# A convolution with max pooling: the first casting load doubled to half an image, and the hand-written program order laid out anew

## The chip, the core and the metric

The kernel runs on one core of a Trainium2 chip. The metric is device time in microseconds (us) of one execution. Five engines work side by side, each through its own list of instructions in order: PE (matrix multiply; PEld is its weight load), DVE (vector), ACT (scalar), POOL (GpSimd) and SP, which here only issues DMA transfers. POOL issues transfers too. They meet through semaphores. PE writes its results to PSUM, of which this kernel has eight banks in two sets of four.

## The reference

A 3x3 convolution with padding 1 over 16 images of 64 channels and 64x64 pixels to 128 channels, and a 2x2 maximum over the result:

```python
batch, c_in, h, w, c_out, k = 16, 64, 64, 64, 128, 3
for each b, co, ci, kh, kw:
    conv[b, co] += weight[co, ci, kh, kw] * x_pad[b, ci, kh:kh+h, kw:kw+w]
output[b, c, i, j] = np.max(conv[b, c, 2*i:2*i+2, 2*j:2*j+2])
```

All inputs and outputs are float32; the kernel multiplies in bfloat16.

## The kernel before

**Tiles.** Images are taken two at a time: the 64 channels of one lie in partitions 0 to 63, those of the other in 64 to 127 (h is 0 or 1 below). A pair of images is cut into four chunks of 16 rows, each giving 8 pooled rows. There are 32 chunks, of two kinds, in an order fixed by `SEQ`: 14 of kind K and 18 of kind W. The vertical maximum needs an upper and a lower row of the convolution. In both kinds the kernel splits them into a part that both share and two remainders: it takes the maximum of the remainders and adds the shared part after that.

**Kind K** holds x in bfloat16 (tiles `kx`, a whole pair of images each, three buffers). Its products are PAa and PAb (first remainder), PBa and PBb (second remainder) and PR (shared part). Only PR needs a tile made beforehand, `KS` (sum of two rows, DVE). **Kind W** holds x in float32 (tiles `wx`, three buffers of four chunks) and needs four row tiles: S (sum, DVE), Z and Y (differences, POOL) and E (a difference: `E.i` makes it on DVE, `e.i` on POOL). Its products are P2 and P0 (first remainder), P3 (second) and P1 (shared part). After P2, `SE` on ACT seeds the second remainder's bank with the negated first one.

**A product** is three matmuls of 64x128 weights with 8x64 columns, for one h. Two products, one for each h, are issued interleaved, and they run at the same time on the two halves of PE. The order holds 142 such pairs; 852 matmuls in all.

**After the products** of a chunk: EV/ev (ACT) copies the first remainder out of PSUM, MX/mx (DVE) takes the maximum of it and the second, in the second's bank, PR or P1 is added there, OD/od (ACT) copies odd columns out, CM/cm (DVE) takes the maximum over columns into the tile `o`, and with the second h SP stores it. Capital letters stand for K, small ones for W. A PSUM bank goes back to its set after EV/ev or CM/cm, and the next product that needs a bank takes the one given back first in program order.

**Loads.** `wload` (L110 to L117, issued by SP) brings a W chunk as it is, 480 to 576 KB. `kload` (L104 to L108, issued by POOL) brings K chunks and casts to bfloat16 on the way. The first two K chunks are instead loaded in float32 by SP (`kfirst` L124, `ksecond` L335) and cast on DVE (XO, XE) and ACT (X1 and X2, L344). In the order `LD.i` is the load of W chunk i and `L0`, `L1`, ... the next casting load. Before, L0 is chunk 2 alone, L1 chunk 3 alone, and L2 to L6 are half images of two chunks each. SP issues loads and stores in one list, so a load waits behind the stores that stand ahead of it, and these for their CM/cm.

**The order** is written out by hand in `ORDER`: every engine gets its instructions in the order in which the names stand there. A name's *slot*, below, is the number of product pairs that stand ahead of it. Two rules add waits: a row tile on POOL waits for the DVE row operation that stands last ahead of it (`on_gpsimd`), and LD.1, LD.2, LD.3 wait for GM, E.0, E.1 (`load_w`), as ksecond waits for D2. At the start the 3x3 weights are combined (g0 to GP), turned by PE (T...) and copied to `wt` (V...).

Of the kernel before, what the change touches and what calls it, by code (L numbers as in the profile page):

```python
# [11 lines left out]
def kernel(  # L12
# [370 lines left out]


    ORDER = """
        g2 D0 D2 g1 TD0 GS g0 TD2 KX2 VD0 TG2 VD2 TG0 L0 VG2 TG1 XO GM VG0 PAa.0.0+PAa.0.1 XE LD.1 TGM GP
# [4 lines left out]
        P1.0.0+PAb.2.1 MX.1.0 SE.1.1 LD.3 P0.1.0+PBa.2.1 LD.4 EV.2.1 L2 E.2 P3.1.0+PBb.2.1 od.0.0 ev.1.0 S.1
        PR.1.0+P0.1.1 cm.0.0 Z.2 PAa.2.0+P2.2.1 MX.2.1 OD.1.0 ev.1.1 P2.2.0+P3.1.1 mx.1.0 Y.2 SE.2.1 CM.1.0
        PAb.2.0+PR.2.1 mx.1.1 SE.2.0 P1.1.0+P0.2.1 OD.2.1 E.3 EV.2.0 P0.2.0+P1.1.1 S.2 ev.2.1 P3.2.0+P3.2.1
        ev.2.0 CM.2.1 Y.3 PAa.3.0+PBa.1.1 od.1.0 mx.2.1 od.1.1 PAb.3.0+PAa.3.1 cm.1.0 Z.3 cm.1.1
        PBa.2.0+P1.2.1 mx.2.0 EV.3.0 PBb.2.0+PAb.3.1 LD.6 S.4 LD.5 P1.2.0+PBb.1.1 KS.3 Y.4 PAa.4.0+PBa.3.1
        od.2.0 MX.1.1 EV.3.1 PAb.4.0+PBb.3.1 cm.2.0 e.4 MX.2.0 P2.3.0+PR.1.1 EV.4.0 MX.3.1 PBa.3.0+PAa.4.1
        od.2.1 OD.1.1 Z.4 cm.2.1 SE.3.0 PBb.3.0+PAb.4.1 CM.1.1 PR.2.0+PR.3.1 EV.4.1 MX.3.0 P0.3.0+P2.3.1
        KS.4 OD.2.0 OD.3.1 CM.2.0 PR.3.0+PBa.4.1 L3 SE.3.1 S.3 P2.4.0+PBb.4.1 OD.3.0 CM.3.1 Z.5 ev.3.0
        CM.3.0 P3.3.0+P0.3.1 MX.4.1 SE.4.0 PBa.4.0+P2.4.1 LD.8 ev.3.1 S.6 P0.4.0+P3.3.1 LD.7 e.5 mx.3.0
        SE.4.1 PBb.4.0+PR.4.1 ev.4.0 mx.3.1 P3.4.0+P0.4.1 Y.6 MX.4.0 P1.3.0+P3.4.1 ev.4.1 mx.4.0  # L400
        PAa.5.0+P1.3.1 Z.6 od.3.0 mx.4.1 OD.4.1 PR.4.0+P2.5.1 cm.3.0 CM.4.1 PAb.5.0+P1.4.1 Y.5 OD.4.0 od.3.1
        CM.4.0 P2.5.0+PAa.5.1 od.4.1 cm.3.1 EV.5.0 P1.4.0+PAb.5.1 cm.4.1 SE.5.0 E.6 PBa.5.0+PBa.5.1 od.4.0
        KS.5 SE.5.1 cm.4.0 P0.5.0+PBb.5.1 EV.5.1 S.8 P2.6.0+P0.5.1 ev.5.0 LD.9 S.5 PBb.5.0+P2.6.1 SE.6.0 Z.7
        MX.5.1 P3.5.0+P3.5.1 ev.5.1 MX.5.0 P0.6.0+PR.5.1 SE.6.1 mx.5.0 e.7 PR.5.0+P3.6.1 ev.6.0 mx.5.1
        P1.5.0+P0.6.1 OD.5.1 Y.7 OD.5.0 CM.5.1 P2.7.0+P1.5.1 CM.5.0 od.5.0 ev.6.1 cm.5.0 PAa.6.0+PAa.6.1 L4
        KS.6 od.5.1 SE.7.0 PAb.6.0+P2.7.1 mx.6.1 Z.8 cm.5.1 P3.6.0+PAb.6.1 EV.6.0 P0.7.0+P1.6.1 S.9 EV.6.1
        LD.10 PBa.6.0+PBa.6.1 e.8 mx.6.0 od.6.1 SE.7.1 P3.7.0+PBb.6.1 cm.6.1 ev.7.0 PBb.6.0+P0.7.1 S.7 Y.8
        MX.6.1 PAa.7.0+P2.8.1 ev.7.1 mx.7.0 P1.6.0+P3.7.1 SE.8.1 MX.6.0 Y.9 PAb.7.0+PR.6.1 od.6.0 mx.7.1
        P1.7.0+P0.8.1 OD.6.1 cm.6.0 Z.9 PR.6.0+P3.8.1 CM.6.1 od.7.0 ev.8.1 cm.7.0 P2.8.0+P1.7.1 LD.11 EV.7.0
        mx.8.1 PAa.8.0+PAa.7.1 OD.6.0 SE.8.0 CM.6.0 PAb.8.0+P1.8.1 KS.8 od.7.1 KS.7 P0.8.0+PAb.7.1 od.8.1  # L410
        E.10 EV.8.0 PBa.7.0+PBa.7.1 Z.10 cm.8.1 ev.8.0 cm.7.1 PBb.7.0+PBb.7.1 EV.7.1 P2.10.0+PAa.8.1 MX.7.0
        e.9 LD.12 P3.8.0+P2.10.1 MX.7.1 SE.10.0 PR.7.0+PAb.8.1 Y.10 SE.10.1 mx.8.0 P0.10.0+PR.7.1 OD.7.0
        EV.8.1 CM.7.0 P1.8.0+P0.10.1 S.10 OD.7.1 L5 ev.10.0 P2.9.0+PBa.8.1 CM.7.1 od.8.0 S.11
        P3.10.0+PBb.8.1 ev.10.1 cm.8.0 PBa.8.0+P2.9.1 Z.12 MX.8.1 SE.9.0 PBb.8.0+P3.10.1 mx.10.0 LD.13
        SE.9.1 e.11 P3.9.0+PR.8.1 MX.8.0 P0.9.0+P3.9.1 mx.10.1 OD.8.1 Z.11 PR.8.0+P0.9.1 CM.8.1 ev.9.0
        P1.10.0+P1.10.1 mx.9.0 ev.9.1 e.12 PAa.9.0+P2.11.1 mx.9.1 od.10.1 od.10.0 PAb.9.0+PAa.10.1 OD.8.0
        cm.10.1 cm.10.0 P1.9.0+PAb.10.1 EV.9.0 KS.11 KS.9 PBa.9.0+PBa.10.1 EV.10.1 CM.8.0 Y.11
        P2.11.0+P1.9.1 od.9.0 SE.11.1 cm.9.0 PBb.9.0+PBb.10.1 od.9.1 Y.13 SE.11.0 cm.9.1 PAa.10.0+P0.11.1
        MX.10.1 PAb.10.0+P2.12.1 ev.11.1 LD.15 KS.10 MX.9.0 P0.11.0+P3.11.1 LD.14 e.13 SE.12.1
        P3.11.0+PR.10.1 ev.11.0 mx.11.1 PR.9.0+P0.12.1 L6 OD.10.1 EV.10.0 Z.13 CM.10.1 PBa.10.0+P1.11.1  # L420
        mx.11.0 OD.9.0 PBb.10.0+PAa.9.1 od.11.1 CM.9.0 ev.12.1 Y.12 cm.11.1 P1.11.0+PAb.9.1 MX.10.0
        P2.12.0+PAa.11.1 od.11.0 EV.9.1 cm.11.0 PR.10.0+PAb.11.1 S.13 SE.12.0 P2.13.0+P3.12.1 OD.10.0 Y.14
        EV.11.1 CM.10.0 P0.12.0+P2.13.1 mx.12.1 SE.13.0 P3.12.0+PBa.9.1 LD.16 ev.12.0 S.12 P0.13.0+PBb.9.1
        SE.13.1 e.14 mx.12.0 PAa.11.0+P1.12.1 MX.9.1 P1.12.0+P0.13.1 S.14 od.12.1 P3.13.0+PR.9.1 Z.14
        cm.12.1 od.12.0 ev.13.0 cm.12.0 PAb.11.0+P3.13.1 ev.13.1 P2.14.0+PBa.11.1 e.15 OD.9.1 mx.13.1
        EV.11.0 PBa.11.0+P2.14.1 CM.9.1 SE.14.0 mx.13.0 PBb.11.0+PBb.11.1 Y.15 SE.14.1 LD.17 P0.14.0+P1.13.1
        MX.11.0 P3.14.0+P0.14.1 Z.16 MX.11.1 ev.14.0 PR.11.0+P3.14.1 ev.14.1 mx.14.0 e.16 P1.13.0+PR.11.1
        od.13.1 mx.14.1 OD.11.0 P1.14.0+PAa.12.1 CM.11.0 od.13.0 cm.13.1 Z.15 P2.15.0+P1.14.1 cm.13.0
        od.14.0 OD.11.1 cm.14.0 PAa.12.0+P2.16.1 od.14.1 CM.11.1 Y.16 SE.15.0 PAb.12.0+PAb.12.1 cm.14.1
        PBa.12.0+PBa.12.1 EV.12.0 S.16 P0.15.0+PBb.12.1 EV.12.1 S.15 P2.16.0+PAa.13.1 SE.16.1 KS.12 ev.15.0  # L430
        PBb.12.0+PAb.13.1 e.17 MX.12.1 SE.16.0 P3.15.0+P0.16.1 MX.12.0 EV.13.1 Z.17 P0.16.0+P3.16.1 ev.16.1
        mx.15.0 P3.16.0+P2.17.1 ev.16.0 mx.16.1 Y.17 P1.15.0+PR.12.1 SE.17.1 mx.16.0 PR.12.0+P1.16.1 OD.12.1
        od.15.0 CM.12.1 PAa.13.0+P0.17.1 OD.12.0 cm.15.0 od.16.1 PAb.13.0+P3.17.1 S.17 ev.17.1 cm.16.1
        P1.16.0+P2.15.1 EV.13.0 KS.13 CM.12.0 P2.17.0+PBa.13.1 od.16.0 mx.17.1 SE.15.1 PBa.13.0+PBb.13.1
        cm.16.0 SE.17.0 PBb.13.0+P0.15.1 MX.13.1 P0.17.0+P3.15.1 ev.15.1 MX.13.0 P3.17.0+P1.17.1 mx.15.1
# [59 lines left out]
```

## Time and profile before

| | us |
|---|---|
| three timed runs | 114.47, 114.31, 111.48 |
| their median | 114.31 |
| the profiled execution, its own time | 112.98 |
| span of the profiled execution, first to last instruction | 111.2 |
| time that lies around the span (112.98 - 111.2) | 1.78 |

In the profile a line such as "L263 DVE TENSOR_TENSOR ws<-wx" names the code line, the engine, the operation and the tiles (output, arrow, inputs). Names in the profile are those of tiles: `ws`, `wz`, `wy`, `we` and `ks` are the row tiles S, Z, Y, E/e and KS; `o` is CM/cm; L302 is MX/mx. Busy time is not a bound by itself: what counts is where PE, which does the least avoidable work, stands still, and for what.

### The profile page before, as it was taken

What the parts mean: (1) busy time and instruction counts of PE and PEld (TensorE: products, weight loads), DVE (VectorE), ACT (ScalarE), POOL (GpSimd) and SP (SyncE); (2) the same over time, 40 slices, a digit from 0 to 9 for tenths busy, and PEclk for the clock granted to TensorE, in tenths of its full rate; (3) what the DMA queues carried; (4) which work ended last, traced back from release to release, by engine and by line L of the source; (5) the groups of instructions that cost most, each with busy time, mean ns of one, the idle gap of its engine ahead of it and who ended that gap; (6) DMA issues with size and microseconds to landing.
All of it is one profiled execution on the core that took longest, in us unless ns stands there. A gap on an engine that the chain in (4) does not pass through costs nothing.

```text
span 111.2 us, 2480 instructions
## 1 busy us (share of the span) xinstructions
PE 100.8 (91%) x889; PEld 50.2 (45%) x889; DVE 92.2 (83%) x177; ACT 79.4 (71%) x173; POOL 67.6 (61%) x76
## 2 busy tenths in 40 slices
PE   7997999999999988799999998299999999999930
PEld 2552355544444433355568552144444454555400
DVE  0597489889999996999998898238989999989960
ACT  4574698864797796587797957097896877989640
POOL 6329137826947960995938649386918999690000
PEclk9999999999999999999999999999999999999999
DMA  3989937897899999549988889739699595400534
GB/s 89 352 212 221 320 67 152 221 273 221 245 304 126 281 359 304 173 110 143 316 182 278 205 113 268 262 113 168 212 262 291 223 215 218 136 0 6 189 140 143
DMA packets 12781, 22.55 MB, mean 203 GB/s; under 512 B 992, under 2 KB 9312, under 8 KB 12768
## 3 DMA queue, kind: packets, MB, share of 16 engines
q1 hardware_dynamic: 11760, 19.24, 55.1%
q0 software_dynamic: 1008, 3.15, 18.1%
q8 instruction: 7, 0.11, 0.5%
q14 instruction: 6, 0.05, 0.2%
HBM read 17.14 MB, written 8.39 MB: 230 GB/s over the span
## 4 chain that ended last, share of the span: by engine, by line
PE 39%; DMA 17%; DVE 9%; POOL 3%; issue 2%; ACT 1%; SPq 0%; DVEq 0%; POOLq 0%
PE acc L213 39%; DMA wx<-in_x_dram 8%; DMA kx<-in_x_dram 8%; DVE acc L302 3%; DVE ws L263 3%; DVE o L315 2%; POOL wz L263 1%; POOL we L263 1%; POOL wy L263 1%; DVE ks L263 1%; ACT od L306 1%; DVE we L263 1%; SPq L327 0%; DVEq L490 0%; POOLq L263 0%
## 5 line engine op out<-in xcount | busy, mean ns | idle before, releaser
L213 PEld LDWEIGHTS <-wt 64*128 64x128 bf16 x852 | 46.8, 94 | 51.6 <-issue 5.9
L213 PE MATMUL acc<-kx,wt 64*128 64x512 bf16 (+3 forms) x336 | 62.0, 374 | 3.6 <-DMA kx<-in_x_dram 2.6
L293 ACT COPY ev<-acc 128x512 f32<-128x512 f32 x64 | 36.7, 596 | 11.0 <-PE acc L213 10.6
L302 DVE TENSOR_TENSOR acc<-acc,ev 128x512 f32<-128x512 f32 x64 | 42.1, 692 | 2.7 <-PE acc L213 1.3
L263 POOL TENSOR_TENSOR wz<-wx 128x512 bf16<-128x512 f32 x18 | 23.4, 1302 | 18.6 <-DVE we L263 6.4
L213 PE MATMUL acc<-we,wt 64*128 64x504 bf16 (+1 forms) x108 | 28.4, 376 | 0.8 <-DVE o L315 0.8
L263 POOL TENSOR_TENSOR wy<-wx 128x512 bf16<-128x512 f32 x18 | 23.5, 1309 | 8.7 <-DVE ws L263 3.1
L213 PE MATMUL acc<-wz,wt 64*128 64x504 bf16 (+1 forms) x108 | 28.1, 377 | 0.0
L306 ACT COPY od<-acc 128x256 f32<-128x256 f32 x64 | 22.8, 382 | 7.4 <-PE acc L213 7.0
L315 DVE TENSOR_TENSOR o<-acc,od 128x256 f32<-128x256 f32 x64 | 24.7, 416 | 3.6 <-ACT od L306 3.2
L213 PE MATMUL acc<-ws,wt 64*128 64x504 bf16 (+1 forms) x108 | 26.7, 377 | 0.1
L213 PE MATMUL acc<-wy,wt 64*128 64x504 bf16 (+1 forms) x108 | 26.0, 377 | 0.0
L298 ACT ACTIVATE acc<-acc 128x512 f32<-128x512 f32 x36 | 21.0, 589 | 4.5 <-PE acc L213 2.3
L213 PE MATMUL acc<-ks,wt 64*128 64x504 bf16 (+1 forms) x84 | 20.2, 377 | 0.7 <-DVE acc L302 0.7
L263 DVE TENSOR_TENSOR ws<-wx 128x512 bf16<-128x512 f32 x18 | 15.9, 891 | 1.3 <-DMA wx<-in_x_dram 1.3
L263 POOL TENSOR_TENSOR we<-wx 128x512 bf16<-128x512 f32 x12 | 15.3, 1272 | 2.6 <-DVE ks L263 2.0
L263 DVE TENSOR_TENSOR ks<-kx 128x512 bf16<-128x512 bf16 x14 | 6.3, 462 | 3.5 <-DMA kx<-in_x_dram 2.9
L263 DVE TENSOR_TENSOR we<-wx 128x512 bf16<-128x512 f32 x6 | 5.5, 909 | 0.9 <-DMA wx<-in_x_dram 0.9
L442 PE MATMUL acc<-const-bfloat16-1.0 128*128 128x512 bf16 x8 | 3.6, 625 | 0.8 <-PEq L476 0.8
L108 POOL DMA_DIRECT2D kx<-in_x_dram x7 | 4.3, 610 | 0.0
L174 PEld LDWEIGHTS <-wq 128*128 128x128 bf16 x28 | 2.2, 120 | 1.6 <-issue 1.2
L174 PE MATMUL acc<-ident,wq 128*128 128x128 bf16 x28 | 2.7, 263 | 0.0
(28 smaller groups left out, 15.5 us busy)
## 6 DMA issues: line engine op xcount, KB each, us to landing
out_dram<-o SPq DMA_DIRECT2D x30, 256.0 KB, 4.5
wx<-in_x_dram SPq DMA_DIRECT2D x8, 512.0 KB, 6.8
wx<-in_x_dram SPq DMA_DIRECT2D x5, 480.0 KB, 5.8
wx<-in_x_dram SPq DMA_DIRECT2D x4, 544.0 KB, 6.0
kx<-in_x_dram POOLq DMA_DIRECT2D x3, 528.0 KB, 8.1
...
```

What stands on the lines that cost most here:

```text
L108: nc.gpsimd.dma_start(out=ktile(i)[:, lo:hi, :], in_=rows_of(p, lo, hi))
L174: nc.tensor.transpose(tp[:, (j - lo) * 128 : (j - lo + 1) * 128], wq[:, j : j + 2, :].rearrange("a b c -> a (b c)"), ident,)
L213: lambda kw=kw, o0=o0, o1=o1, c0=c0, c1=c1: nc.tensor.matmul(dst[:, i0:i1, o0:o1], wt[lo : lo + CI, m0 + kw - h, :], rows(lo, i0, i1, c0, c1),
L263: return engine.tensor_tensor(out=r, in0=t[:, f + a : f + a + 2 * R - 1 : 2, :], in1=t[:, f + b : f + b + 2 * R - 1 : 2, :], op=op,)
L293: nc.scalar.copy(out=ev[g], in_=acc[g[2]][ta[g]])
L298: nc.scalar.mul(acc[h][t], acc[h][ta["w", i, h]], -1.0)
L302: nc.vector.tensor_tensor(out=t, in0=t, in1=ev.pop(g), op=MAX)
L306: nc.scalar.copy(out=od[g], in_=acc[g[2]][tb[g]][:, :, 1::2])
L315: nc.vector.tensor_tensor(out=o[:, h], in0=acc[h][tb[g]][:, :, 0::2], in1=od.pop(g), op=MAX)
L442: warm = nc.tensor.matmul(acc[n % 2][n // 2], ones[:, 0:128], ones, start=True, stop=True, skip_group_check=True)
```

## The change

L0 becomes the half image of chunks 2 and 3, in one transfer; the casting loads are then six, L0 to L5, each of two chunks. `ORDER` is written anew throughout. Two further row differences move from POOL to DVE: E on DVE for chunks 0, 1, 2, 5, 10, 13, 15 and 17 (before: 0, 1, 2, 3, 6 and 10). All else, products and row tiles alike, is the same work.

```diff
-    def kload_next(n):
-        if n < 2:
-            kload(n + 2)
-        else:
-            i = 2 * n
-            kload(i, min(2, NK - i))
+    def load_k(n):
+        kload(2 * n + 2, min(2, NK - 2 * n - 2))
...
-        "L": kload_next,
+        "L": load_k,
...
     ORDER = """
-        g2 D0 D2 g1 TD0 GS g0 TD2 KX2 VD0 TG2 VD2 TG0 L0 VG2 TG1 XO GM VG0 PAa.0.0+PAa.0.1 XE LD.1 TGM GP
-        PAb.0.0+PAb.0.1 VGM E.0 PBa.0.0+PBa.0.1 EV.0.0 KS.0 LD.2 P2.0.0+PBb.0.1 EV.0.1 Z.0 VG1 TGP MX.0.1
-        PBb.0.0+P2.0.1 X1 Y.0 VGP SE.0.1 PAa.1.0+PR.0.1 MX.0.0 X2 PAb.1.0+P0.0.1 S.0 L1 SE.0.0 PR.0.0+P3.0.1
-        KS.1 ev.0.1 KS.2 P0.0.0+PAa.1.1 EV.1.0 mx.0.1 OD.0.0 P3.0.0+PAb.1.1 ev.0.0 E.1 PBa.1.0+P1.0.1 OD.0.1
+        D2 g0 D0 g1 TD2 KX2 g2 TD0 GS VD2 TG0 TG2 VG0 TG1 XO VD0 VG2 PAa.0.0+PAa.0.1 GM XE PAb.0.0+PAb.0.1
+        LD.1 GP PBa.0.0+PBa.0.1 VG1 EV.0.1 L0 KS.0 PBb.0.0+PBb.0.1 EV.0.0 E.0 TGM MX.0.1 TGP Z.0 LD.2 VGM
+        MX.0.0 X1 P2.0.0+P2.0.1 VGP Y.0 PR.0.0+PR.0.1 SE.0.0 PAa.1.0+PAa.1.1 OD.0.0 S.0 SE.0.1
+        P0.0.0+PAb.1.1 E.1 OD.0.1 X2 P3.0.0+P0.0.1 CM.0.1 LD.3 Z.1 ev.0.0 CM.0.0 PAb.1.0+P3.0.1 EV.1.1
+        mx.0.0 P2.1.0+P2.1.1 ev.0.1 LD.4 KS.1 PBa.1.0+PBa.1.1 EV.1.0 S.1 SE.1.1 PBb.1.0+PBb.1.1 L1 mx.0.1
...
```

On POOL's own list L0 stands in the same place as before, right behind the sum `gsum` (GS). The slots of some loads and of what first needs them, counted in `ORDER`:

| load | before: slot | first need, slot | after: slot | first need, slot |
|---|---|---|---|---|
| LD.1 | 1 | E.1, 10 | 2 | E.1, 8 |
| LD.5 | 27 | Z.5, 37 | 20 | Z.5, 36 |
| LD.6 | 27 | S.6, 39 | 32 | e.6, 43 |
| LD.7 | 40 | Z.7, 52 | 33 | S.7, 48 |
| LD.8 | 39 | S.8, 50 | 38 | S.8, 55 |
| LD.13 | 84 | Y.13, 94 | 83 | E.13, 98 |
| K chunks 2 (and 3) | 0 (L0) | KS.2, 8 | 3 (L0) | KS.2 and PAa.2.1, 16 |
| K chunks 4, 5 | 15 (L2) | PAa.4.0, 28 | 13 (L1) | KS.4, 34 |
| K chunks 6, 7 | 36 (L3) | PAa.6.0, 57 | 35 (L2) | PAa.6.0, 51 |
| K chunks 8, 9 | 58 (L4) | PAa.8.0, 70 | 57 (L3) | KS.8, 72 |
| K chunks 10, 11 | 80 (L5) | PAa.10.1, 89 | 80 (L4) | PAa.10.0, 92 |
| K chunks 12, 13 | 99 (L6) | PAa.12.1, 119 | 98 (L5) | PAa.12.0, 119 |

More of the change, by code (lines that the diff above doesn't have):

```diff
@@ L385 @@
     ORDER = """
-        g2 D0 D2 g1 TD0 GS g0 TD2 KX2 VD0 TG2 VD2 TG0 L0 VG2 TG1 XO GM VG0 PAa.0.0+PAa.0.1 XE LD.1 TGM GP
-        PAb.0.0+PAb.0.1 VGM E.0 PBa.0.0+PBa.0.1 EV.0.0 KS.0 LD.2 P2.0.0+PBb.0.1 EV.0.1 Z.0 VG1 TGP MX.0.1
-        PBb.0.0+P2.0.1 X1 Y.0 VGP SE.0.1 PAa.1.0+PR.0.1 MX.0.0 X2 PAb.1.0+P0.0.1 S.0 L1 SE.0.0 PR.0.0+P3.0.1
-        KS.1 ev.0.1 KS.2 P0.0.0+PAa.1.1 EV.1.0 mx.0.1 OD.0.0 P3.0.0+PAb.1.1 ev.0.0 E.1 PBa.1.0+P1.0.1 OD.0.1
-        EV.1.1 mx.0.0 Z.1 P2.1.0+PAa.2.1 od.0.1 CM.0.0 PBb.1.0+P2.1.1 CM.0.1 SE.1.0 cm.0.1 Y.1
@@ L391 @@
[L391 to L435, printed above, removed]
@@ L436 @@
-        ev.17.0 PR.13.0+PR.13.1 mx.17.0 od.17.1 cm.17.1 OD.13.0 P1.17.0+P1.15.1 OD.13.1 CM.13.0 CM.13.1
-        od.17.0 od.15.1 cm.17.0 cm.15.1
+        D2 g0 D0 g1 TD2 KX2 g2 TD0 GS VD2 TG0 TG2 VG0 TG1 XO VD0 VG2 PAa.0.0+PAa.0.1 GM XE PAb.0.0+PAb.0.1
+        LD.1 GP PBa.0.0+PBa.0.1 VG1 EV.0.1 L0 KS.0 PBb.0.0+PBb.0.1 EV.0.0 E.0 TGM MX.0.1 TGP Z.0 LD.2 VGM
+        MX.0.0 X1 P2.0.0+P2.0.1 VGP Y.0 PR.0.0+PR.0.1 SE.0.0 PAa.1.0+PAa.1.1 OD.0.0 S.0 SE.0.1
+        P0.0.0+PAb.1.1 E.1 OD.0.1 X2 P3.0.0+P0.0.1 CM.0.1 LD.3 Z.1 ev.0.0 CM.0.0 PAb.1.0+P3.0.1 EV.1.1
@@ new lines @@
+        mx.0.0 P2.1.0+P2.1.1 ev.0.1 LD.4 KS.1 PBa.1.0+PBa.1.1 EV.1.0 S.1 SE.1.1 PBb.1.0+PBb.1.1 L1 mx.0.1
+        SE.1.0 Y.1 P1.0.0+P0.1.1 MX.1.1 P0.1.0+P1.0.1 MX.1.0 ev.1.1 P3.1.0+P3.1.1 KS.2 ev.1.0 KS.3
+        PR.1.0+PAa.2.1 od.0.0 mx.1.1 Z.2 PAa.2.0+PR.1.1 cm.0.0 OD.1.0 od.0.1 CM.1.0 PAb.2.0+P1.1.1 OD.1.1
+        cm.0.1 PBa.2.0+PAb.2.1 E.2 od.1.1 EV.2.0 LD.5 S.2 PBb.2.0+PAa.3.1 EV.2.1 e.3 cm.1.1 PAa.3.0+PAb.3.1
+        MX.2.0 PAb.3.0+PBa.2.1 mx.1.0 Y.2 P2.2.0+PBb.2.1 CM.1.1 EV.3.0 P1.1.0+P2.2.1 EV.3.1 S.3 SE.2.0
@@ new lines @@
+        PR.2.0+PBa.3.1 Y.3 MX.2.1 SE.2.1 P0.2.0+PBb.3.1 od.1.0 OD.2.0 cm.1.0 P3.2.0+P0.2.1 ev.2.0 Z.3 CM.2.0
+        P2.3.0+PR.2.1 mx.2.0 ev.2.1 PBa.3.0+P3.2.1 MX.3.1 OD.2.1 e.4 SE.3.0 P1.2.0+P2.3.1 CM.2.1 mx.2.1
+        PBb.3.0+PR.3.1 Y.4 SE.3.1 LD.6 P0.3.0+P1.2.1 MX.3.0 OD.3.1 LD.7 P3.3.0+P3.3.1 CM.3.1 ev.3.0 KS.4
+        PR.3.0+P0.3.1 od.2.0 S.4 L2 od.2.1 PAa.4.0+PAa.4.1 cm.2.0 Z.5 OD.3.0 cm.2.1 ev.3.1 PAb.4.0+PAb.4.1
+        mx.3.0 P2.4.0+P2.4.1 LD.8 CM.3.0 Z.4 EV.4.0 mx.3.1 P1.3.0+PBa.4.1 EV.4.1 SE.4.0 PBa.4.0+PBb.4.1 E.5
@@ new lines @@
+        SE.4.1 P0.4.0+P1.3.1 S.5 od.3.0 PBb.4.0+P0.4.1 Y.5 cm.3.0 ev.4.0 MX.4.1 P2.5.0+P3.4.1 od.3.1 MX.4.0
+        ev.4.1 e.6 P3.4.0+PR.4.1 SE.5.0 cm.3.1 mx.4.1 PR.4.0+P2.5.1 OD.4.1 Z.6 LD.9 CM.4.1 P0.5.0+PAa.5.1
+        OD.4.0 mx.4.0 SE.5.1 P3.5.0+PAb.5.1 CM.4.0 ev.5.0 KS.5 P1.4.0+P3.5.1 S.7 LD.10 PAa.5.0+P0.5.1 od.4.0
+        mx.5.0 Z.7 EV.5.1 PAb.5.0+P1.4.1 ev.5.1 P1.5.0+P2.6.1 od.4.1 e.7 cm.4.1 PAa.6.0+PBa.5.1 od.5.0
+        cm.4.0 SE.6.1 PAb.6.0+PBb.5.1 mx.5.1 Y.6 EV.5.0 P2.6.0+P0.6.1 EV.6.0 MX.5.1 PBa.6.0+P1.5.1 cm.5.0
@@ new lines @@
+        ev.6.1 S.8 PBa.5.0+PR.5.1 od.5.1 S.6 SE.6.0 PBb.6.0+PAa.6.1 cm.5.1 L3 PBb.5.0+PAb.6.1 KS.6 MX.6.0
+        Y.8 P3.6.0+P2.7.1 EV.6.1 MX.5.0 P0.6.0+P3.6.1 OD.5.1 CM.5.1 e.8 PR.6.0+PBa.6.1 ev.6.0 mx.6.1
+        PR.5.0+PBb.6.1 SE.7.1 mx.6.0 Y.7 OD.6.0 P2.7.0+P1.6.1 OD.5.0 CM.6.0 P1.6.0+P0.7.1 CM.5.0 SE.7.0
+        MX.6.1 e.9 PAa.7.0+P3.7.1 od.6.1 LD.11 ev.7.1 P0.7.0+PR.6.1 od.6.0 mx.7.1 Y.9 PAb.7.0+PAa.7.1 OD.6.1
+        cm.6.0 ev.7.0 CM.6.1 P3.7.0+PAb.7.1 KS.7 EV.7.0 P2.8.0+P1.7.1 Z.8 EV.7.1 mx.7.0 PBa.7.0+P2.8.1
@@ new lines @@
+        cm.6.1 od.7.1 SE.8.0 cm.7.1 P1.7.0+PBa.7.1 E.10 SE.8.1 LD.12 PBb.7.0+PBb.7.1 od.7.0 KS.8
+        P0.8.0+P0.8.1 Z.10 MX.7.0 P3.8.0+P2.10.1 cm.7.0 ev.8.0 MX.7.1 P2.9.0+P3.8.1 ev.8.1 Z.9 mx.8.0
+        PR.7.0+PR.7.1 SE.10.1 mx.8.1 SE.9.0 P1.8.0+P0.10.1 Y.10 OD.7.1 OD.7.0 P0.9.0+P1.8.1 CM.7.1 ev.10.1
+        CM.7.0 P3.9.0+P2.9.1 S.9 od.8.1 ev.9.0 PAa.8.0+PAa.8.1 cm.8.1 L4 od.8.0 mx.9.0 SE.9.1
+        PAb.8.0+PAb.8.1 e.11 cm.8.0 P2.10.0+P3.10.1 EV.8.1 P1.9.0+P0.9.1 EV.8.0 S.10 LD.13 LD.14
@@ new lines @@
+        PBa.8.0+P3.9.1 mx.10.1 SE.10.0 Z.11 LD.15 od.9.0 PBb.8.0+PBa.8.1 ev.9.1 cm.9.0 P0.10.0+P1.10.1 e.12
+        mx.9.1 P3.10.0+P2.11.1 MX.8.0 od.10.1 ev.10.0 P2.11.0+PBb.8.1 Y.11 cm.10.1 mx.10.0 SE.11.1
+        PR.8.0+P1.9.1 SE.11.0 S.11 P1.10.0+P0.11.1 OD.8.0 MX.8.1 P3.11.0+P3.11.1 Z.12 ev.11.1 CM.8.0
+        P0.11.0+PR.8.1 od.9.1 mx.11.1 od.10.0 Y.12 PAa.10.0+P2.12.1 cm.10.0 OD.8.1 ev.11.0 cm.9.1
+        PAb.10.0+P1.11.1 CM.8.1 mx.11.0 PBa.10.0+PAa.10.1 od.11.1 EV.10.0 S.12 PAa.9.0+PAa.9.1 LD.16 cm.11.1
@@ new lines @@
+        PAb.9.0+PAb.9.1 KS.9 KS.10 PBa.9.0+PAb.10.1 L5 KS.11 EV.9.1 E.13 PBb.9.0+PBa.10.1 EV.9.0 S.13
+        EV.10.1 P1.11.0+PBa.9.1 MX.9.0 Y.13 P2.12.0+PBb.10.1 od.11.0 SE.12.1 cm.11.0 PBb.10.0+PBb.9.1
+        MX.10.1 SE.12.0 Z.13 PR.9.0+P0.12.1 LD.17 MX.9.1 P0.12.0+P3.12.1 ev.12.1 MX.10.0 e.14 P3.12.0+PR.9.1
+        ev.12.0 mx.12.1 PR.10.0+PR.10.1 OD.9.0 mx.12.0 Y.14 OD.9.1 P2.13.0+P1.12.1 CM.9.1 OD.10.0 OD.10.1
+        CM.9.0 P1.12.0+P2.14.1 CM.10.0 od.12.1 Z.14 cm.12.1 PAa.11.0+PAa.11.1 od.12.0 CM.10.1 SE.14.1
@@ new lines @@
+        PAb.11.0+PAb.11.1 cm.12.0 SE.13.0 E.15 PBa.11.0+P2.13.1 EV.11.1 S.14 PBb.11.0+P0.14.1 EV.11.0 e.16
+        SE.13.1 P0.13.0+P3.14.1 MX.11.0 ev.14.1 P2.14.0+P0.13.1 ev.13.0 Y.16 mx.14.1 P3.13.0+PBa.11.1
+        SE.14.0 PR.11.0+PBb.11.1 mx.13.0 Z.15 P0.14.0+P1.14.1 MX.11.1 OD.11.0 ev.13.1 P3.14.0+P3.13.1
+        CM.11.0 Z.16 od.14.1 ev.14.0 P1.13.0+P2.16.1 cm.14.1 mx.13.1 PAa.12.0+PR.11.1 Y.15 od.13.0 mx.14.0
+        SE.16.1 P2.15.0+P1.13.1 OD.11.1 cm.13.0 P1.14.0+P0.16.1 CM.11.1 od.13.1 SE.15.0 cm.13.1
@@ new lines @@
+        PAb.12.0+PAa.12.1 S.15 ev.16.1 P0.15.0+P2.15.1 EV.12.0 E.17 P3.15.0+P3.16.1 od.14.0 SE.15.1 cm.14.0
+        PAa.13.0+PAb.12.1 S.17 PBa.12.0+P0.15.1 mx.16.1 EV.12.1 ev.15.0 PBb.12.0+P3.15.1 KS.12 S.16 ev.15.1
+        PAb.13.0+PBa.12.1 mx.15.0 Z.17 P2.16.0+PBb.12.1 EV.13.0 MX.12.0 P1.15.0+P1.16.1 SE.16.0 mx.15.1
+        PR.12.0+PAa.13.1 MX.12.1 od.15.0 P0.16.0+PAb.13.1 cm.15.0 OD.12.0 od.16.1 CM.12.0 P3.16.0+P1.15.1
+        ev.16.0 cm.16.1 P2.17.0+PR.12.1 KS.13 EV.13.1 mx.16.0 Y.17 od.15.1 PBa.13.0+P2.17.1 OD.12.1 SE.17.0
@@ L438 @@
+        CM.12.1 PBb.13.0+PBa.13.1 cm.15.1 SE.17.1 P0.17.0+PBb.13.1 MX.13.0 P3.17.0+P0.17.1 ev.17.0 MX.13.1
+        P1.16.0+P3.17.1 mx.17.0 ev.17.1 PR.13.0+PR.13.1 od.16.0 mx.17.1 cm.16.0 OD.13.1 P1.17.0+P1.17.1
+        OD.13.0 CM.13.1 CM.13.0 od.17.1 od.17.0 cm.17.1 cm.17.0
     """
```

## The prediction, made before the changed kernel was run

> **What bounds the kernel now.** I read the page first, then the timeline of PE, then the chain that ended last, then the DMA issues and the timelines of DVE and POOL around each hole of PE.
>
> ```profile
> span 111.2 us, 2480 instructions
> PE 100.8 (91%) x889; PEld 50.2 (45%) x889; DVE 92.2 (83%) x177; ACT 79.4 (71%) x173; POOL 67.6 (61%) x76
> ...
> q1 hardware_dynamic: 11760, 19.24, 55.1%
> q0 software_dynamic: 1008, 3.15, 18.1%
> ```
>
> PE leads. In its timeline one pair of products starts 0.65 us after the other (66.49, 67.14), so 142 pairs take 92.0 us at 0.648. The first starts at 6.11 and the last ends near 106.5: PE lost 8.4 us between (parts below: 8.8, since a few pairs start 0.08 early). From the starts of the pairs: 2.4 us before 13.71 (start-up), 0.40 between 24 and 27, 2.12 between 40.55 and 47.2, 2.91 between 67.8 and 72.0, 0.95 later. The table of stages shows the two large holes:
>
> ```profile
> 13.70:40.50 26.80, 26.79 (x248) 12.93 (x247) 25.11 (x49) 21.22 (x49) 18.63 (x16) 1.00 0.85 221
> 40.50:47.20 6.70, 5.28 (x44) 2.34 (x41) 5.62 (x11) 4.33 (x10) 2.88 (x4) 1.00 0.78 253
> 47.20:67.80 20.60, 20.59 (x193) 12.31 (x193) 19.42 (x37) 16.38 (x36) 14.44 (x13) 1.00 0.83 190
> 67.80:72.00 4.20, 1.62 (x13) 0.43 (x11) 2.00 (x6) 1.07 (x4) 2.75 (x3) 1.00 0.87 309
> ```
>
> The second column is the stage's length, the third PE's busy time: 1.4 and 2.6 us short there, nothing elsewhere. The chain names what ended them:
>
> ```profile
> 33.74 9.37 DMA wx<-in_x_dram
> ...
> 62.44 9.08 DMA kx<-in_x_dram
> ```
>
> First hole: LD.8 was issued at 33.74, at its slot (39, PE was there at 34.06), and took 9.37 us, but S.8 on DVE needs it 11 slots (7.1 us) later; DVE stood 1.08 us and PE lost 0.99 + 0.22. The other 0.91 there is E.6 on DVE, which ran into POOL's row operations, 1.0 us late by then (Y.5 started at 39.58, its slot at 38.6):
>
> ```profile
> 39.56 1.83 DVE L263 TENSOR_TENSOR we<-wx 128x512 bf16<-128x512 f32 x1
> 41.31 0.41 DVE L263 TENSOR_TENSOR ks<-kx 128x512 bf16<-128x512 bf16 x1
> 41.65 0.41 DVE L315 TENSOR_TENSOR o<-acc,od 128x256 f32<-128x256 f32 x1
> 43.13 1.29 DVE L263 TENSOR_TENSOR ws<-wx 128x512 bf16<-128x512 f32 x2 [1.08 <-DMA wx<-in_x_dram]
> ```
>
> Alone the same operation takes 0.69. Second hole: the casting load of chunks 10 and 11, issued at 62.44 (slot 80), is needed 9 slots (5.8 us) later and took 9.08.
>
> What makes transfers long is the casting load. Window 33.5 to 36.5, right after the one issued at 31.35:
>
> ```profile
> q0 software_dynamic: 85, 0.34, 85.8%
> q1 hardware_dynamic: 35, 0.03, 3.5%
> ```
>
> SP's queue q1, with two loads and three stores issued and not landed, got 3.5% of the DMA engines. Loads of wx issued at 33.74, 34.77 and 64.8 (2.4 to 3.4 us after a casting load) took 9.37, 9.52 and 8.98; those issued ahead of one (17.28, 17.79, 59.69, 75.68, 76.15) 5.5 to 6.8. Half-image casting loads took 6.06 alone (48.33) and 8.1 to 9.1 beside others. Last reading: SP and POOL issue each load from LD.3 and L2 on within 0.8 us of PE's arrival at its slot. So slots times 0.648 may be set against transfer times.
>
> **The change, part by part.** *Late loads.* By slots, LD.5 to LD.8 now have 16, 11, 15 and 17 slots (10.4, 7.1, 9.7, 11.0 us). LD.6, the shortest, stands three slots (1.9 us) ahead of L2, and so among the 5.5 to 6.8 us; what waits for it is e.6 on POOL, needed by PE only at slot 50. LD.8 stands three slots behind L2: 6.4 (issued at 50.05, 1.7 us behind a casting load) to 9.5, under 11.0. The first hole goes: -2.12 (bounds -2.12 and -1.2, if another E meets POOL). Its 0.40 at 24 to 27 hangs on E.3 waiting 0.95 us for LD.3; E moves to POOL with 12 slots: -0.40 (0 to -0.40). Casting loads of 4 to 9 get 21, 16 and 15 slots (13.6, 10.4, 9.7 us), over 9.1. Of chunks 10 and 11: 12 slots, 7.8 us. Against 6.06 to 9.08 PE waits 0 to 1.3; LD.13 to 15 come right behind as in the crowded cases, so I take 8.6, a wait of 0.8: -2.91 + 0.8.
>
> *Start.* L0 keeps its place on POOL (before: issue 5.37, landing 13.38), but reads 992 KB instead of 512. 480 KB more, at q1's rate (19.24 MB in 55.1% of 111.2 us, 314 GB/s), are 1.56 us. LD.1 (6.50 to 13.58 before, about 6.85 now, since GM stands later on DVE) waits behind it: landing 15.1, bounds 13.58 (unharmed) and 16.4 (6.85 + 9.52). E.1 stands on DVE ahead of CM.0.1, which gives back the bank of P2.1.1. So P2.1 starts at 15.1 + 0.69 + 0.4 = 16.2. It is the pair of slot 10, which started at 15.00 before: +1.2 (bounds -0.3 and +2.5). What is ahead costs less: TGM and TGP now stand behind PBb.0, and P2.0 waits for VGM on ACT (0.6 us), but PAa.1 finds two more products done when ksecond lands (10.55 before; issued some 0.45 earlier, D2 being first on DVE), so PE reaches slot 10 at 14.2 to 15.3 without E.1. KS.2, KS.3 and PAa.2.1 need L0 at slot 16, over 4 us after 15.1.
>
> *Engines.* Two E from POOL (1.27 each) to DVE: 0.60 (its step there) and a collision each, 0.20 on average (S and E took 21.4 us for 24, against 16.6 at 0.69): 1.6 us of DVE, which is idle 17% of the span. Between 0 and 1.6 reach the end; half, +0.8. POOL loses 2.5 us and one issue of 0.58: 61% busy, nothing. Tail: four half stores end it again, and W15's whole store is no longer the fifth; 0 to -0.5, I take 0. The 0.95 of small holes I leave.
>
> Sum: 111.2 - 2.12 - 0.40 - 2.91 + 0.8 + 1.2 + 0.8 = 108.6, and 1.78 around it: **110.4 us**. That stands against the profiled execution's 112.98, which lies 1.33 under the median of 114.31; against the median it is 3.4% less.
>
> **Rivals.** *B, the start is unharmed and the casting load is in time:* without the +1.2 and 0.8, and with -0.3, 108.1. For it: q0 had 56% and q1 43% from 8 to 10.5, a milder split than at 33.5. The Trainium skill, "DMA: Bandwidth & Descriptors", "Queues, rings and completion order", has each DMA engine go round robin between queues packet by packet. By that rule LD.1 would lose little and B hold; the 3.5% above speaks against it.
>
> *C, DVE takes over:* after 13.7 DVE was busy 84.2 us (stages added). After E.1 it has, with KS.1 and two E more, 85.6 left. From 15.8 that ends at 101.4 without a pause; before, DVE idled 10.0 us after 13.7, 4.4 for transfers. With the other 5.5 it ends at 106.9 against 107.9 before: span 110.2, 112.0; with a late transfer more, to 113.5. Against it: many of those pauses were PE's holes passed on.
>
> *D, slower, by collisions:* 11 of 38 row operations on DVE were lengthened by one of POOL's; the worst, E.6, by 1.14. There are 26 S and E now. If the new places raise the mean from 0.20 by 0.24, 6.2 us are added and 116.6 reached, 2% over the median; at 0.5 each it is 118. It breaks even with the profiled execution at 0.10 more. The skill's "SBUF — State Buffer", on the shared port pair, says that a DVE instruction with two SBUF inputs and a GpSimd one that reads SBUF exclude each other for the whole instruction; E.6, which lasted until Y.5 had ended, agrees. Against D: POOL's rows wait for DVE's by `on_gpsimd`, and collisions came mostly where POOL was late.
>
> **Numbers.** Forecast (109 to 112) 0.45, B 0.15, C 0.25, D 0.15. Range 108.1 to 113.5: it leaves out D and the edges. A measurement of this kernel can tell about 2% (its own runs lie 2.7% apart). Faster by that: under 112.0, the forecast and B nearly whole, 0.58; within, C, 0.27; slower, D, 0.15.
>
> **What would show it.** Right: no hole of PE over 0.5 us between 20 and 50 us; one under 1.5 us at PAa.10, ended by a `kx` transfer; E.1 on DVE waiting for `wx` until about 15, and P2.1 at about 16. Wrong: LD.1 landing by 13.6 (B); DVE over 90% busy after 16 us with PE waiting for `o` or `acc` (C); S and E above 1.1 us on average (D); or a casting load with 9 us or more of slots that still ends a hole.

## The result, and the profile after

| | before, us | after, us |
|---|---|---|
| timed runs | 114.47, 114.31, 111.48, 113.0 | 106.75, 107.11, 106.93, 107.43 |
| median | 113.66 | 107.02 |
| the profiled execution: span / own time | 111.2 / 112.98 | 105.0 / 106.75 |

After over before is 0.954, with an interval of 95% from 0.942 to 0.966. This ratio, like the ratios below, goes by the runs within 1.5% of the fastest of each kernel (of before 111.48 and 113.0), and so leaves out one profiled execution among the experiments, new_L0_late, that ran at a granted clock of 0.66 and took 152.2 us. The direction was forecast; the size in us was not: 107.0 lies below the range of 108.1 to 113.5. As a share the miss is smaller: the range is 0.946 to 0.993 of the 114.31 that the prediction had, and 0.954 lies in it.

The head of the page of after, and its two lines of the DMA queues:

```profile
span 105.0 us, 2492 instructions
...
PE 99.1 (94%) x888; PEld 53.7 (51%) x889; DVE 89.4 (85%) x179; ACT 78.5 (75%) x173; POOL 63.3 (60%) x73
...
q1 hardware_dynamic: 11760, 19.24, 53.6%
q0 software_dynamic: 864, 3.15, 19.0%
```

All bytes are the same as before. The only count that fell is that of casting packets, from 1008 to 864: 144 for each casting load, whether it brings a quarter of an image or half of one.

The span of after cut into start, middle and end (columns as in the table of stages of before: length, then PE, PEld, DVE, ACT and POOL busy, clock, DMA share, GB/s):

```profile
0.00:18.20 18.20, 16.70 (x126) 8.14 (x128) 11.92 (x25) 11.61 (x22) 8.91 (x27) 1.00 0.78 228
18.20:100.70 82.50, 82.40 (x763) 45.60 (x761) 76.64 (x153) 66.28 (x151) 54.41 (x46) 1.00 0.73 213
100.70:105.00 4.30, 0.00 (x0) 0.00 (x0) 0.85 (x3) 0.60 (x2) 0.00 (x0) 0.99 0.52 183
```

In 82.5 us PE stands still for 0.1. Before, PE lost 8.4 us between its first pair and its last; here it loses 2.3, by the starts of the pairs, and all of it before 18.2. The chain that ended last says the same:

```profile
8.96 0.34 PE acc L174 x4
9.30 0.02 issue
9.32 0.61 ACT wt L185
9.93 0.05 issue
9.98 1.47 PE acc L213 x12
11.45 0.26 issue
11.70 88.09 PE acc L213 x809
```

One piece of products, 88 us long, leads to the end, and no transfer is in the chain any more. Before, transfers held 17% of it, the two pieces of 9.37 and 9.08 us among them. The largest loss left is 1.2 us at 8.8 to 10: PE turns GM (TGM, 0.34) and P2.0 waits for its copy VGM (L185, 0.61), as the prediction said it would (0.6), though its sum has no charge for it.

### The profile page after: what moved, and what is told of

Same layout as the page of the kernel before. It is cut to its first block, busy times and chain, and to the rows that moved or that the text cites. A ratio compares the mean times of both kernels' runs of the same rounds, so it can differ in the third digit from the quotient of the medians.

```text
span 105.0 us, 2492 instructions
## 1 busy us (share of the span) xinstructions
PE 99.1 (94%) x888; PEld 53.7 (51%) x889; DVE 89.4 (85%) x179; ACT 78.5 (75%) x173; POOL 63.3 (60%) x73
## 4 chain that ended last, share of the span: by engine, by line
PE 94%; ACT 1%; issue 0%; DVE 0%; DVEq 0%
PE acc L213 89%; PE acc L438 3%; PE acc L174 2%; ACT wt L185 1%; DVE o L315 0%; ACT od L306 0%; DVEq L486 0%
## 5 line engine op out<-in xcount | busy, mean ns | idle before, releaser
L213 PEld LDWEIGHTS <-wt 64*128 64x128 bf16 x852 | 50.3, 94 | 42.2 <-issue 1.5
L213 PE MATMUL acc<-kx,wt 64*128 64x512 bf16 (+3 forms) x336 | 54.7, 373 | 0.3 <-issue 0.3
L293 ACT COPY ev<-acc 128x512 f32<-128x512 f32 x64 | 35.6, 594 | 9.8 <-PE acc L213 9.5
L213 PE MATMUL acc<-wz,wt 64*128 64x504 bf16 (+1 forms) x108 | 26.8, 377 | 0.0
L213 PE MATMUL acc<-we,wt 64*128 64x504 bf16 (+1 forms) x108 | 26.1, 377 | 0.5 <-ACT wt L185 0.5
L213 PE MATMUL acc<-wy,wt 64*128 64x504 bf16 (+1 forms) x108 | 24.3, 377 | 0.0
L213 PE MATMUL acc<-ks,wt 64*128 64x504 bf16 (+1 forms) x84 | 18.8, 377 | 0.0
L263 POOL TENSOR_TENSOR we<-wx 128x512 bf16<-128x512 f32 x10 | 12.7, 1269 | 3.4 <-DVE ws L263 2.9
L263 DVE TENSOR_TENSOR ws<-wx 128x512 bf16<-128x512 f32 x18 | 13.5, 752 | 0.0
L108 POOL DMA_DIRECT2D kx<-in_x_dram x6 | 3.6, 594 | 0.0
```

Source lines behind the costliest of these rows:

```text
L213: lambda kw=kw, o0=o0, o1=o1, c0=c0, c1=c1: nc.tensor.matmul(dst[:, i0:i1, o0:o1], wt[lo : lo + CI, m0 + kw - h, :], rows(lo, i0, i1, c0, c1),
L263: return engine.tensor_tensor(out=r, in0=t[:, f + a : f + a + 2 * R - 1 : 2, :], in1=t[:, f + b : f + b + 2 * R - 1 : 2, :], op=op,)
L293: nc.scalar.copy(out=ev[g], in_=acc[g[2]][ta[g]])
```

## The experiments

Times are medians in us; "before" is the same kernel on the chip of that call (113.29, 112.61 and 113.74 in the three calls), and after itself, run again in the third, gave 106.93 (106.52 to 107.25 in six runs). Before scatters between 109.5 and 115.1 over all its runs, after between 106.5 and 107.4, so what is built on after can be read to a few tenths, what is built on before only to one or two us. The fastest runs of before, 109.5 to 109.8 in two of the calls, also say that the gain isn't always 6 us: against them it is under 3.

**The theory and its rivals.** The theory: the gain is the loads that now stand early enough, so that no transfer ends a wait of PE; the half-image L0 and the engines have little part in it. Rivals: the half image itself brings it; the rest of the order does; the time won was taken from DVE. Later experiments set rivals for what was missed: what L0 costs at the start, and what makes a casting load long. Each expectation names its own theories.

### The two parts of the change apart

*Before's order with the half image* (old_order_half): L1 struck out of `ORDER`, and

```diff
     def kload_next(n):
-        if n < 2:
-            kload(n + 2)
-        else:
-            i = 2 * n
-            kload(i, min(2, NK - i))
+        i = 2 * max(n, 1)
+        kload(i, min(2, NK - i))
```

> The order of before, with L0 as the half image of chunks 2 and 3 in its old place and L1 left out; nothing else. Theory 1 (the gain comes from loads that stand early enough for their transfer): the two holes of PE at 40 to 47 and 68 to 72 us stay, the time is that of before within -0.5 and +1.5 us (LD.1 may land up to 1.5 us later). Theory 2 (the one large casting load is what helps, since the second small one no longer holds up SP's queue at 13 to 16 us): 108 to 110 us.

Measured: 113.59 (111.05 to 114.11), no difference from before that these runs can tell, and none of the four in the 108 to 110 of theory 2: the rival that the half image alone brings the gain falls. Of the holes the second stays (2.9 us at slot 90), and of the first the half at slot 50 (0.8); the half that LD.8 caused (slot 54) is not in this profile. The waits of PE in it, the longest first (total, times, longest):

```profile
PE acc L213 <- DMA kx<-in_x_dram: 2.8, 1, 2.8
```

and the same transfer's time, in its chain of waits, is before's to the hundredth:

```profile
61.86 9.08 DMA kx<-in_x_dram
```

*After's order with L0 as two casting loads* (new_order_split), one behind the other:

```diff
-        kload(2 * n + 2, min(2, NK - 2 * n - 2))
+        if n == 0:
+            kload(2)
+            kload(3)
+        else:
+            kload(2 * n + 2, min(2, NK - 2 * n - 2))
```

> The kernel after, with L0 issued as two casting loads, chunk 2 and right behind it chunk 3. Theory 1: 107 us, within 0.7. Theory 2: 109 us or more.

Measured: 107.30 (106.88 to 107.52), ratio to before 0.945 (0.940 to 0.949). The order carries the change; the half image is worth 0.3 us here, about what these runs scatter by.

### Before, with only a few loads moved

*LD.8 and LD.7 from slots 39 and 40 to slot 33* (old_w_early), nothing else:

```diff
-  PBa.4.0+P2.4.1 LD.8 ev.3.1 S.6 P0.4.0+P3.3.1 LD.7 e.5 mx.3.0
+  PBa.4.0+P2.4.1 ev.3.1 S.6 P0.4.0+P3.3.1 e.5 mx.3.0
...
-  CM.1.1 PR.2.0+PR.3.1
+  CM.1.1 LD.8 LD.7 PR.2.0+PR.3.1
```

> The order of before with LD.8 and LD.7 alone moved from slots 39 and 40 to slot 33, ahead of the casting load L3. Theory 1: both land in 5.5 to 6.8 us, the hole of PE at 40 to 47 us goes and 2.1 us with it, the hole at 68 stays (now near 66): about 111 us on a chip where before takes 113. Theory 3 (an old order mended in one place gives the time back in the next, because DVE is nearly full): under 0.7 us gained.

Measured: 110.22 (109.03 to 113.71), ratio 0.961 (0.955 to 0.967), which rests on 109.03 and 109.10 alone. The two loads took 9.07 and 9.74 us, not the 5.5 to 6.8 of theory 1 (a casting load was issued within 0.4 us of both), but they landed at 39.6 and 40.8, in time: the part of the first hole at slot 54 is gone. The 0.8 at slot 50 stays. The second hole was only 0.8 long in the profiled execution: the same casting load, from the same slot, took 6.95 this time.

*The same, and LD.12 from slot 76 to 70, the casting load of chunks 10 and 11 from slot 80 to 74* (old_wk_early):

```diff
-  e.9 LD.12 P3.8.0+P2.10.1
+  e.9 P3.8.0+P2.10.1
...
-  S.10 OD.7.1 L5 ev.10.0
+  S.10 OD.7.1 ev.10.0
...
-  mx.8.1 PAa.8.0+PAa.7.1
+  mx.8.1 LD.12 PAa.8.0+PAa.7.1
...
-  PBa.7.0+PBa.7.1 Z.10
+  PBa.7.0+PBa.7.1 L5 Z.10
```

> As the run with LD.8 and LD.7 early, and besides LD.12 from slot 76 to 70 and the casting load L5 (chunks 10 and 11) from slot 80 to 74. Theory 1: the second hole goes too, 5 us in all: about 108 us, most of what the new order brings. Theory 3: 110.5 us or more, with the hole moved to another wait.

Measured: 108.65 (107.97 to 108.86), ratio 0.956 (0.951 to 0.961). The casting load took 9.45 and came in time all the same. Four loads in other places bring most of what the whole new order brings; its four runs lie within 0.9 us, those of old_w_early within 4.7. By the ratios, whose intervals overlap, LD.7 and LD.8 bring the larger part of that, and the other two loads mainly take away the long runs. In its profile PE loses 4.2 us, against 2.3 in after: 2.8 at the start, where after loses the 2.3, then 0.6 at slots 42 to 50, 0.65 at slot 109 and 0.4 at the last pair. The one at slot 109 is a collision, here a piece of the chain, where S runs beside a row operation of POOL (Y, from 78.13 to 79.39):

```profile
78.34 1.60 DVE ws L263
```

*LD.12 alone from slot 76 to 70* (old_LD12_early), the two lines of LD.12 in the diff above:

> The order of before, with LD.12 alone moved from slot 76 to 70, so that it has landed, or nearly, when the casting load L5 is issued (slot 80). L5 is where it was. Theory 1: L5 takes 6.2 to 7.2 us instead of 9.08, the hole of PE at 68 us shrinks from 2.75 to 0.3 to 1.4 us, 1.4 to 2.5 us gained on before. Theory 2: L5 still takes 8.5 us or more and the time is that of before within 0.7.

Measured: 109.89 (109.79 to 110.92). The median of before in this call is 113.74, but its fastest run took 109.47, so the time alone shows no gain. The casting load of chunks 10 and 11, with its neighbours, by the DMA issues of 59 to 63 us (KB each, us from issue to landing), first before, then this kernel:

```profile
wx<-in_x_dram SPq DMA_DIRECT2D x1, 544.0 KB, 5.7
kx<-in_x_dram POOLq DMA_DIRECT2D x1, 496.0 KB, 9.1
```

```profile
kx<-in_x_dram POOLq DMA_DIRECT2D x1, 496.0 KB, 6.8
```

The casting load was left where it was and took 2.3 us less, and PE's hole there is 0.62 instead of 2.75 (2.91 by the prediction's count), as theory 1 has it. But that LD.12's place did it is not shown. LD.12, issued at 55.59, landed at 62.02, after the casting load's issue at 61.62, so the same 1056 KB of SP's were under way at that moment as before, a load and two stores. And old_w_early had the casting load short (6.95) with LD.12 in its old place, 2.7 us from landing. This transfer's length differs from one execution to another where nothing near it was moved, and what decides on it stays open.

### The start

*L0 waits for E.0* (new_L0_late), so that LD.1 goes out alone:

```diff
-        kload(2 * n + 2, min(2, NK - 2 * n - 2))
+        behind(kload(2 * n + 2, min(2, NK - 2 * n - 2)), mark["E0"] if n == 0 else None)
```

with `kload` returning its transfer, and L0 behind E.0 in `ORDER`.

> The kernel after, with L0 alone moved on POOL: it waits for E.0 (about 8.7 us instead of 5.4). It asks what L0 takes from LD.1, the step of the prediction that failed (+1.56 us of landing forecast, +0.27 seen). Theory 1 (L0 still takes DMA time from LD.1): LD.1 lands at 12.0 to 12.8 instead of 13.85, E.1 no longer waits, 106.2 to 106.7 us. Theory 2 (LD.1 lands late by its own queue, behind ksecond, and L0 costs it next to nothing): LD.1 lands at 13.5 or later, 107 within 0.4; and if L0 lands after 18.5 us, the wait moves to KS.2 and PAa.2.1 and the time is 107.5 or more.

Measured: 106.19 (106.09 to 106.38 in three runs; the fourth is the 152.2 us named above). That is 0.7 to 0.8 less than after in the other call, and than new_rows_pool and new_loads_close (107.03 and 106.94), which have after's start, in the same call. So L0 does cost LD.1 something, as theory 1 has it. Its own profile is that of the 152.2 us; the kernel below issues L0 as late, and there E.1 no longer waits for LD.1, which took 4.2 and 4.4 us in its two profiles instead of 7.3. The DMA issues of 5 to 8 us in the second:

```profile
wx<-in_x_dram SPq DMA_DIRECT2D x1, 512.0 KB, 4.4
```

*Besides this, TGM ahead of PBa.0, VGM ahead of EV.0.1, TGP and VGP right ahead of PR.0* (new_start, and the same kernel again as new_start_2):

```diff
-  GP PBa.0.0+PBa.0.1 VG1 EV.0.1 KS.0
+  GP TGM PBa.0.0+PBa.0.1 VG1 VGM EV.0.1 KS.0
...
-  E.0 L0 TGM MX.0.1 TGP Z.0 LD.2 VGM
-  MX.0.0 X1 P2.0.0+P2.0.1 VGP Y.0 PR.0.0+PR.0.1
+  E.0 L0 MX.0.1 Z.0 LD.2
+  MX.0.0 X1 P2.0.0+P2.0.1 Y.0 TGP VGP PR.0.0+PR.0.1
```

> As the run with L0 late, and besides the middle weight block GM is turned two pairs earlier (TGM ahead of PBa.0, VGM on ACT ahead of EV.0.1; TGP and VGP right ahead of PR.0), so that P2.0 doesn't wait for it. Theory 1: the hole of 1.2 us ahead of P2.0 goes, LD.1 is early, and P2.1 starts at 13.6 to 14.0 instead of 14.62: 106.0 to 106.4 us. Theory 2: E.1 still waits for LD.1, nothing gained over the run with L0 late.

> The run with L0 late and GM turned early once more, beside the kernel after on the same chip: if its start is worth what the traces say (P2.1 at 13.71 instead of 14.62), it is 0.8 to 1.1 us faster than the kernel after.

Measured: 106.04 (105.53 to 106.25), and 105.83 (105.59 to 106.15) beside 106.93 of after: 1.0% less than after, with no run of one inside the runs of the other. This version beats both kernels. Against L0 late alone (106.19) the step is 0.15 in the same call, within the scatter. Its chain of waits:

```profile
9.18 1.31 DVE acc L302 x2
10.49 0.04 issue
10.54 88.09 PE acc L213 x815
```

The piece of products starts 1.2 us earlier than in after (11.70). What is left ahead of it is MX on DVE, 1.0 us, and 0.4 at slot 2, behind TGM.

### DVE

*After with E.13, E.15 and E.17 given back to POOL* (new_rows_pool):

```diff
-  E.13
+  e.13
...
-  E.15
+  e.15
...
-  E.17
+  e.17
```

> The kernel after, with E.13, E.15 and E.17 made on POOL (e) in the same places. The prediction charged 0.4 us of the end for each E on DVE. Theory A (DVE decides there): 0.8 to 1.2 us less, 105.9 to 106.3. Theory B (DVE's work is hidden as long as no transfer is late): 107.0 within 0.3.

Measured: 107.03 (106.85 to 107.53), the same as after. What these E cost DVE is hidden, with PE short of nothing; and three more row operations on POOL (1.27 each) hurt as little.

### What makes a casting load long

*After with LD.13 to LD.15 from slots 83 and 84 to right behind L4* at slot 80 (new_loads_close), so that 1760 KB of loads and stores go out in the 2.5 us behind it:

```diff
-  cm.8.1 L4 od.8.0
+  cm.8.1 L4 LD.13 LD.14 LD.15 od.8.0
```

> The kernel after, with LD.13, LD.14 and LD.15 moved from slots 83 and 84 to right behind the casting load L4 (slot 80). It asks what made L4 take 6.17 us where 8.6 was forecast. Theory 1 (what SP issues within some 2 us of a casting load is moved with it and lengthens it): L4 takes 8.5 us or more, PAa.10.0 waits 0.7 to 1.5 us, 107.7 to 108.5 us. Theory 2 (a casting load's length does not hang on that): L4 6 to 6.5 us, 107.0 within 0.3.

*After with the same three loads moved to slot 75, ahead of L4* (new_loads_ahead):

```diff
-  EV.8.0 S.10 LD.13 LD.14
-  PBa.8.0+P3.9.1 mx.10.1 SE.10.0 Z.11 LD.15 od.9.0
+  EV.8.0 S.10
+  PBa.8.0+P3.9.1 mx.10.1 SE.10.0 Z.11 od.9.0
...
-  PR.7.0+PR.7.1 SE.10.1
+  LD.13 LD.14 LD.15 PR.7.0+PR.7.1 SE.10.1
```

> The kernel after, with LD.13, LD.14 and LD.15 (1.5 MB) moved from slots 83 and 84 to slot 75, ahead of the casting load L4 (slot 80). Theory 1 (a casting load is long when SP's transfers issued ahead of it have not landed): L4 takes 8.3 us or more instead of 6.2, PAa.10.0 waits 0.3 to 1.7 us, 107.3 to 108.7 us. Theory 2 (it was long for another reason, such as the stores around it): L4 stays under 6.8 us, no hole, 107.0 within 0.4.

Their yardstick, after run again (after_again):

> The kernel after, unchanged, on the chip of this call, as the yardstick for the other three: 107.0 us within 0.5.

Measured: loads close behind 106.94 (106.79 to 107.06), no change, so a crowd behind is not what lengthens this load; loads ahead 107.70 (107.37 to 107.87), 0.77 more than after run again. The DMA issues of 58 to 62 us, first close behind, then ahead:

```profile
wx<-in_x_dram SPq DMA_DIRECT2D x2, 512.0 KB, 7.5
...
kx<-in_x_dram POOLq DMA_DIRECT2D x1, 496.0 KB, 6.4
wx<-in_x_dram SPq DMA_DIRECT2D x1, 480.0 KB, 8.6
```

```profile
out_dram<-o SPq DMA_DIRECT2D x2, 256.0 KB, 9.2
kx<-in_x_dram POOLq DMA_DIRECT2D x1, 496.0 KB, 9.5
```

The casting load takes 6.4 with the crowd behind it and 9.5 with the crowd ahead; in the first it is the loads behind it that suffer (7.2 to 8.6 instead of 5.8 to 7.0 in after). How the DMA engines were shared from 59 to 62 us (packets, MB, share of the 16 engines), close behind first, then ahead:

```profile
q0 software_dynamic: 35, 0.14, 54.3%
q1 hardware_dynamic: 90, 0.12, 12.3%
```

```profile
q1 hardware_dynamic: 304, 0.87, 94.6%
```

In the second no packet of the casting load, issued at 59.01, had moved by 62; its first came at about 63. And PE waits for it again, as the chain of that kernel shows:

```profile
59.01 9.52 DMA kx<-in_x_dram
68.53 0.05 issue
68.58 32.00 PE acc L213 x295
```

## Why the prediction was wrong in size and right in kind

The forecast span was 108.6; that of the profiled execution is 105.0. Of the 3.6 us too much, 1.6 are the start (+1.2 forecast, -0.4 measured), 0.8 the casting load, 0.8 the two E, and the other 0.4 what is left of 0.95 of small holes that went as well, net of the rest.

**Late loads: right.** The three removals (2.12, 0.40 and 2.91) came in full: between 18.2 and 100.6 us no pair starts late. The lengths read from the trace held for SP's loads: LD.6 took 5.81 us (5.5 to 6.8 forecast) and LD.8 8.17 (6.4 to 9.5). Setting slots times 0.648 us against the transfer times of the trace was enough to say which waits would end. old_wk_early, with four loads moved and nothing else, reaches 108.65: that shows these places as the cause of most of the gain, and the rest of the new order as the smaller part.

**"LD.13 to 15 come right behind as in the crowded cases, so I take 8.6": this step failed** (+0.8 forecast, 0 measured). L4 took 6.17 (5.99 to 6.43 in seven profiles with this order ahead of it) and had 7.8. I had taken what goes out behind a casting load for what lengthens it. new_loads_close put more behind it and it stayed at 6.4; new_loads_ahead put the same loads ahead of it and it took 9.5. The row that I read (62.44, 9.08) had both: a load and two stores of SP under way, 1056 KB, and a load and two stores behind. The row of 48.33, 6.06 long, had one store ahead and 768 KB behind, and told against me: it wasn't "alone". Over 13 profiles (all but new_L0_late's), of 22 casting loads with at most 800 KB of SP's under way at their issue 13 took under 7.2 us; of 60 with more than 1000 KB, 12 did. That is a tendency and no rule. Two things in the record limit it. L5, the next casting load of after, took 8.5 to 9.7 us in the eight profiles of this order, with only 512 to 992 KB ahead of it; it had 21 slots, 13.6 us, and nobody waited. And the row of 62.44 was not long in the way of new_loads_ahead: its first packet came 1.3 us after the issue, not 4, and it was the last packets that trailed. So what was shown is that loads put ahead can delay a casting load; why the one of before took 9.08 stays open.

**"480 KB more, at q1's rate, are 1.56 us. LD.1 waits behind it": this step failed** (+1.2 forecast, -0.4 measured). The DMA issues of 5 to 7 us, before and then after:

```profile
wx<-in_x_dram SPq DMA_DIRECT2D x1, 512.0 KB, 7.1
kx<-in_x_dram POOLq DMA_DIRECT2D x1, 256.0 KB, 8.0
```

```profile
wx<-in_x_dram SPq DMA_DIRECT2D x1, 512.0 KB, 7.3
kx<-in_x_dram POOLq DMA_DIRECT2D x1, 496.0 KB, 7.7
```

Nearly twice the bytes took 0.3 us less here, and hardly more over all profiles with L0 in this place (256 KB 6.5 to 8.8 us in five, 496 KB 7.6 to 8.3 in six). A casting load keeps the 16 engines busy for 3.3 us in all (19.0% of 105.0 us, over six; before 2.9, 18.1% of 111.2 over seven) and is under way for 6 to 9.5, so its bytes are not its length. The rest of the step held: E.1 waits for LD.1, and P2.1 for E.1, as DVE's timeline of after shows (idle time before it and what ended it, in brackets):

```profile
13.87 0.69 DVE L263 TENSOR_TENSOR we<-wx 128x512 bf16<-128x512 f32 x1 [2.06 <-DMA wx<-in_x_dram]
```

P2.1, the pair of slot 10, starts at 14.62 (the pair of that slot before: 15.00), not at 16.2; in three other profiles with this start (new_rows_pool, new_loads_close, after_again) at 14.76, 14.81 and 15.02. That L0 still costs something shows in new_L0_late (0.7 us less), so the right sum at the start was between nothing and a small gain, with a charge of some 0.7 inside it.

**Two more E on DVE, "half, +0.8": not due.** new_rows_pool moved three E back without a difference. The row operations on DVE became shorter, not longer; the groups of after (count, busy, mean ns, idle before):

```profile
L263 DVE TENSOR_TENSOR ws<-wx 128x512 bf16<-128x512 f32 x18 | 13.5, 752 | 0.0
L263 DVE TENSOR_TENSOR we<-wx 128x512 bf16<-128x512 f32 x8 | 5.8, 728 | 2.1 <-DMA wx<-in_x_dram 2.1
```

Before, the means were 891 and 909. Of 40 row operations 4 were lengthened by one of POOL's, by 1.6 us in all; before, 11 of 38, by 5.6. That fits a POOL that is no longer late, since its inputs are not; no run tests this by itself. The small holes after 80 us, left in the sum at 0.95, went too; whether by the fewer collisions or by the new order is not shown.

**The rivals.** B (start unharmed, casting load in time, 108.1) came nearest, and I gave it 0.15. Its casting load was right and its start nearly so: slot 10 came as early as it said, but LD.1 landed at 13.85, not by 13.6, and L0 does cost it time. It was still 1.3 above the profiled execution's 106.75, by the E charge and the small holes. C, DVE taking over, fell, though half of its sign came true: from 18.2 to 100.7 DVE is busy 76.6 of 82.5 us, 93%, but PE waits for it nowhere there. A high busy share was no bound. D, collisions, went the other way. The rule of the Trainium skill beside D ("SBUF — State Buffer", on the shared port pair) agrees with every collision seen: each of the 11 before and the 4 after began while a row operation of POOL ran, and ended 0.54 to 0.56 us after that one's end (0.28 for the two KS); so did the S of 1.68 us in old_wk_early, of which the chain above has 1.60, against 0.69 alone.

The rule beside B, the Trainium skill's "DMA: Bandwidth & Descriptors", "Queues, rings and completion order" (each DMA engine takes the queues in turn, packet by packet), I had set aside for a share of 3.5%. That share was misread. By packets the turns are much closer: 85 to 35 in the prediction's own window, and 35 against 90 in the window of new_loads_close above, where a casting packet holds an engine for 0.74 us (54.3% of 16 engines for 3 us, over 35) and one of SP's for 0.07. But the rule does not cover it all. Before, from 65.4 to 67.4, with two stores and a load of SP's issued and not landed, the window holds this queue alone:

```profile
q0 software_dynamic: 70, 0.28, 92.2%
```

70 packets to none are no turns, unless SP's packets were not yet ready to go, which the trace does not show. In these stretches the transfer that had been issued first went first, here the casting load, in new_loads_ahead SP's; what decides in general is not shown.
